# Modulation vectors of a two-layer trunk: TensorE sums over partitions replaced by multiply-and-sum instructions of VectorE

## The chip, the cores and the metric

The kernel runs on one core of one Trainium2 chip. A core has TensorE (matrix products, with a weight load that overlaps them), VectorE and ScalarE (elementwise work), POOL (GpSimd) and the queue of SyncE (SP), which issues transfers. They work side by side and wait for each other through semaphores. The metric is the device time of one execution in microseconds. The kernel before took 1705.62 us (median of 3 runs, 1704.53 to 1706.0).

## The reference

The program is a trunk of two layers over 256 context tokens and 256 latent tokens of width 1024. Each layer is a half SwiGLU, a mixer (mLSTM and spatial gating in layer 0, windowed attention in layer 1) and another half SwiGLU. Every one of these is modulated: two conditioning vectors (`c_ctx` for the context tokens, `c` for the latent ones) go through Silu and a 1024 x 9216 matrix per layer, which gives nine vectors of 1024: shift, scale and gate for each of the three parts.

```python
def _modulation(s, w, b):
    m = s @ w + b
    return m.reshape(s.shape[0], N_MOD, 1, D_MODEL)

def _modulate(h, shift, scale):
    return _rms_norm(h) * (1.0 + scale) + shift

def _swiglu(h, w_in, w_out):
    g, u = jnp.split(h @ w_in, 2, axis=-1)
    return (jax.nn.silu(g) * u) @ w_out
...
    sc = jax.nn.silu(c)
    scc = jax.nn.silu(c_ctx)[None]
...
        mod = _modulation(sc, ada_w[layer], ada_b[layer])
        modc = _modulation(scc, ada_w[layer], ada_b[layer])
        h = h + 0.5 * mod[:, 2] * _swiglu(_modulate(h, mod[:, 0], mod[:, 1]), ...)
```

All arithmetic is in fp32. The gates `mod[:, 2]` and `mod[:, 8]` carry a factor 0.5; the scales `mod[:, 1]`, `[:, 4]` and `[:, 7]` carry a 1 added. In layer 1 the context tokens end after the attention, so its vectors 5 to 8 are needed for `c` alone.

## The kernel before

The order of all instructions is written out by hand: a Python class, `Trunk`, emits them in the order in which each engine is to run them. Activations lie with features in partitions and 512 tokens along the row (256 context, 256 latent).

**Weights.** A weight unit is 128 x 1024 numbers (eight 128 x 128 blocks). `pump` streams units in pairs, 1 MB at a time, on SP's queue into a ring of three tiles `raw`, and three more, `rawx`, while there is room. `prep` splits a unit into two parts for a three-product scheme: ScalarE rounds it (`wh`, L259), VectorE takes the rest (`wl`, L243). Both have five buffers. `unit` then issues 24 matmuls, three for each of the eight blocks (L415 to L417). After every second block it calls `sub`.

**SwiGLU.** `ffn` runs three parts of up to eight column blocks `f`. For each `f` there are two units of the first matrix, a Silu on ScalarE (`sg`), a product on VectorE (`hd`), and a split of it into `HH` (ScalarE) and `HL` (VectorE). The part ends with eight units of the second matrix, added into the stream `H` with the gate (L625). The first four units of a SwiGLU, those of `f` 0 and 1, are computed together by `start` or `split_start`.

**Modulation vectors.** The first two vectors of layer 0 are computed on TensorE at the start (`ada`, items "s"). The other 32 items, of 512 outputs each, are spread over the first three half SwiGLUs by `make_ada`. Their weights travel in the same stream, two pieces of 1 MB an item; a piece holds 512 of the 1024 inputs, inputs in partitions and outputs along the row. `sub` calls `vada`, which holds a credit: `vrate` is added at each call (1.0 beside the first matrix, 0.5 beside the second), and one VectorE step costs 1.0. `vload` defines the steps: for each block of 128 inputs and each vector, one multiply-add of 512 columns into the accumulator `va` (L322, the first block L324), with one number of the Silu of `c` per partition. That leaves 128 partial sums per output, one in each partition. `total` sums them on TensorE with a matrix of ones (`pva`, L337), four matmuls for an item; ScalarE copies the result out (L341), and `finish` transposes it on VectorE (L344) and adds the bias with the factor 0.5 (L347). Results go to `mods`.

**POOL** holds a short queue: the masks' load and cast (L500, L501), the powers of the RMS norms (L528, L637 and others) and two more loads (L817, L1208).

Of the kernel before, what the change touches and what calls it, by code (L numbers as in the profile page):

```python
# [9 lines left out]
F32 = mybir.dt.float32  # L10
F32R = mybir.dt.float32r
BF16 = mybir.dt.bfloat16
# [134 lines left out]
class Trunk:  # L147
    def __init__(self, ctx, tc, a):
        self.tc, self.nc, self.a, self.ctx = tc, tc.nc, a, ctx
        self.V, self.S, self.G, self.M = tc.nc.vector, tc.nc.scalar, tc.nc.gpsimd, tc.nc.tensor  # L150
        self.cp = ctx.enter_context(tc.tile_pool(name="cp", bufs=1))
        self.ring = ctx.enter_context(tc.tile_pool(name="ring", bufs=RING))
        self.tp = ctx.enter_context(tc.tile_pool(name="tp", bufs=5))
        self.pp = ctx.enter_context(tc.tile_pool(name="pp", bufs=8, space=PSUM))
        self.dma_ptr = 0
        self.left = [len(v) if k == "u" else 1 for k, v, _, _ in GROUPS]
        self.raw = {}
        self.slot = {}
        self.live = [0, 0]
        self.extra = None  # L160
        self.xs = ExitStack()
        self.where = {}
        for g, (k, v, _, _) in enumerate(GROUPS):
            if k == "u":
                c = 0
                for i in v:
                    self.where[i] = (g, c)
                    c += unit_cols(UNITS[i])
            else:
                self.where[("a",) + v] = (g, 0)  # L170
        self.prep_ptr = 0
        self.half = None
        self.done_ptr = 0
        self.w = {}
        self.pe = [n for n, it in enumerate(ADA) if it[0] != "v"]
        self.ve = [(n, p) for n, it in enumerate(ADA) if it[0] == "v" for p in range(2)]
        self.vops = []
        self.vrate = self.credit = 0.0
        self.folds = []
        self.folded = set()  # L180
        self.posts = []
        self.bg = []
        self.subs = 0
        self.soon = []
        self.rs = {}
        self.adds = []
# [105 lines left out]

    def vada(self):
        self.credit = min(self.credit + self.vrate, 2.0)
        while self.credit >= 1.0:
            if not self.vops:
                if not self.ve:
                    return
                n, p = self.ve[0]
                g = self.where["a", n, p][0]  # L300
                if ADA[n][1][p] > self.done_ptr or g not in self.raw:
                    return
                self.ve.pop(0)
                self.vload(n, p, g)
            self.vops.pop(0)()
            self.credit -= 1.0

    def vload(self, n, p, g):
        V, M = self.V, self.M
        _, _, l, j, c0, w = ADA[n]  # L310
        ss = (1,) if l == 1 and j >= 5 else (0, 1)
        if p == 0:
            self.acc = self.vpool.tile([128, 2, 512], F32, tag="va", name="va", bufs=2)
        acc = self.acc
        raw = self.raw[g]

        def step(x, s):
            k = 4 * p + x
            c = self.SC[:, k, s:s + 1]
            src = raw[:, 512 * x:512 * x + 512]  # L320
            if k:
                V.scalar_tensor_tensor(acc[:, s], src, c, acc[:, s], ALU.mult, ALU.add)  # L322
            else:
                V.tensor_scalar(acc[:, s], src, c, None, ALU.mult)  # L324
            if x == 3 and s == 1:
                self.used(g)
                if p == 1:
                    self.later(wait, wait, total)

        def wait():  # L330
            pass

        def total():
            ps = self.bank("pva")
            sn = len(ss)
            for q in range(4):
                M.matmul(ps[32 * q:32 * q + 32, 0:128 * sn], lhsT=self.ONE[:, 0:32],  # L337
                         rhs=acc[:, ss[0]:2].rearrange("p s (k c) -> p s k c", c=128)[:, :, :, 32 * q:32 * q + 32],
                         start=True, stop=True, skip_group_check=True)
            t0 = self.tmp("va0")  # L340
            self.S.copy(t0[:, 0:128 * sn], ps[:, 0:128 * sn])  # L341

            def finish():
                V.transpose(t0[:, 256:256 + 128 * sn], t0[:, 0:128 * sn])  # L344
                self.folded.add((l, j, c0))
                ks = slice(c0 // 128, (c0 + w) // 128)
                V.scalar_tensor_tensor(  # L347
                    self.MOD[l, j][:, ks, ss[0]:2],
                    t0[:, 256:256 + 128 * sn].rearrange("p (s k m) -> p k s m", s=sn, k=4)[:, :, :, 0], 0.5 if j in (2, 8) else 1.0,
                    self.AB[:, l, j, ks].unsqueeze(2).to_broadcast([128, 4, sn]), ALU.mult, ALU.add)  # L350

            self.later(finish)

        self.vops.extend(lambda x=x, s=s: step(x, s) for x in range(4) for s in ss)

    def later(self, *fns):
        for i, fn in enumerate(fns):
# [102 lines left out]
    def setup(self):  # L460
        nc, a, V, S = self.nc, self.a, self.V, self.S
        cp = self.cp
        self.SM = cp.tile([128, S_N], F32, name="SM")
        self.C = cp.tile([128, C_N], F32, name="C")
        self.A = [None] * KT
        self.SS = cp.tile([128, 512], F32, name="SS")
        self.AX = cp.tile([128, KT, 256], F32, name="AX")
        self.SC = cp.tile([128, KT, 32], F32, name="SC")
        self.ONE = cp.tile([128, 128], F32, name="ONE")
        self.NHF = cp.tile([128, 4], F32, name="NHF")  # L470
        self.IDB = cp.tile([128, 128], BF16, name="IDB")
        self.MKB = cp.tile([128, 2, 128], BF16, name="MKB")
        mods = cp.tile([128, 18, KT, 2], F32, name="mods")
        self.H = cp.tile([128, KT, 512], F32, name="H")
        self.NH = cp.tile([128, KT, 512], F32R, tag="NH", name="NH")
        self.X = [[self.NH[:, k] for k in range(KT)], [None] * KT]
        self.MOD = {(l, j): mods[:, 9 * l + j] for l in range(2) for j in range(9)}
        nc.sync.dma_start(self.SM, a["small"])
        xv = a["xt"].rearrange("(k p) t -> p k t", p=128)
        for k in range(0, KT, 2):  # L480
            nc.sync.dma_start(self.H[:, k:k + 2, :], xv[:, k:k + 2, :])
        nc.sync.dma_start(self.C, a["const"])
        self.widen("f00")
        V.memset(self.ONE, 1.0)
        V.memset(self.NHF, -0.5)
        V.memset(self.SC, 0.0)
        S.activation(self.SC[:, :, 0:2], self.SM[:, S_C:S_C + 16].rearrange("p (k s) -> p k s", s=2), AF.Silu)
        self.AB = self.SM[:, S_AB:S_AB + 144].rearrange("p (l j t) -> p l j t", l=2, j=9)
        V.tensor_scalar(self.AB[:, :, 1::3, :], self.AB[:, :, 1::3, :], 1.0, None, ALU.add)
        V.tensor_scalar(self.AB[:, :, 2::6, :], self.AB[:, :, 2::6, :], 0.5, None, ALU.mult)  # L490
        self.ID = self.C[:, C_ID:C_ID + 128]
        self.heat(HEAT[0])
        for k in range(KT):
            self.add_squares()
            self.square(k, 0, 512)
        V.tensor_copy(self.IDB, self.ID)
# [225 lines left out]
    def ffn(self, l, i, c0, js, jc, jg):  # L722
# [8 lines left out]
        with self.tc.tile_pool(name=f"ffn{l}{i}", bufs=1) as fp:  # L731
            HH = fp.tile([128, 8, n], F32R, name="HH")
            HL = fp.tile([128, 8, n], F32R, name="HL")
            self.vpool = fp
            hs = [[t[:, k] for k in range(8)] for t in (HH, HL)]
            tag = f"f{l}{i}"
            c1 = c0 and c0 - 2
# [15 lines left out]
            ready = dict(zip(STARTS[tag][0], pss))  # L753
            if mid:
                self.masks()

            def proj(u):
                if u in ready:
# [9 lines left out]
            for p, (fa, fb) in enumerate(PARTS):  # L768
                self.vrate = 1.0
                for f in range(fa, fb):  # L770
                    ug, uu = ("wi", l, i, 0, f), ("wi", l, i, 1, f)
                    pg = proj(ug)
                    sg = self.tmp("sg")
# [739 lines left out]
def pack(w):  # L1513
    flat = np.empty(WFLAT, np.float32)
    for k, v, cols, off in GROUPS:
        dst = flat[off:off + cols * 128].reshape(128, cols)
        if k == "u":
            c = 0
            for i in v:
                n = unit_cols(UNITS[i])  # L1520
                b = unit_block(UNITS[i], w)
                dst[:, c:c + n].reshape(b.shape)[:] = b
                c += n
        else:
            _, _, l, j, c0, width = ADA[v[0]]
            kn = 2048 // width
            m = w["ada_w"][l][128 * kn * v[1]:128 * kn * (v[1] + 1), 1024 * j + c0:1024 * j + c0 + width]
            dst.reshape(128, kn, width)[:] = m.reshape(kn, 128, width).transpose(1, 0, 2)
# [15 lines left out]
    mix[:, M_MN:M_MN + 512] = w["mlstm_norm"][0].reshape(1, 512)  # L1544
    xt = np.concatenate([w["ctx"][0].T, w["x"][0].T], axis=1)
    const, late = constants()
    return {"w": flat, "small": small, "mix": mix, "xt": np.ascontiguousarray(xt), "const": const, "late": late}


# [13 lines left out]
```

## Time and profile before

| | |
|---|---|
| runs, median | 1705.62 us |
| profiled execution, its time | 1705.36 us |
| its span, first to last instruction | 1703.2 us |
| TensorE busy | 1689.5 us (99%) |
| VectorE busy | 1143.2 us (67%) |
| ScalarE busy | 652.9 us (38%) |
| POOL busy | 24.7 us (1%) |
| read from HBM | 245.28 MB |
| granted TensorE clock | 0.998 |

A line of a group gives line, engine, operation, written and read tiles, shape and count, then busy time in us and the mean of one in ns, then the idle time of that engine just before them and what ended it. A line of the timeline gives start and duration in us; where several alike are merged, the duration is that of all. Starts of matmuls show more than their durations, since one starts before the last has ended.

### The profile page before, as it was taken

Reading aid. Unit: us, or ns where it says so; the run is one execution under the profiler, and the core shown is the slowest. Engines: PE = TensorE matmul, PEld = TensorE weight load, DVE = VectorE, ACT = ScalarE, POOL = GpSimd, SP = SyncE. Lnnn points to the kernel's source line nnn. Section 1 sums busy time; section 2 is a strip of 40 time slices with the busy share of each in tenths; the row PEclk is TensorE's granted clock in tenths of the full one; section 3 lists DMA queues with packets and bytes.
Section 4 is the critical chain, followed back from the end, with each engine's and each line's share of the span. In section 5 each row is a group of like instructions: output and inputs, shape, how many; then the busy total and the mean of one; then the engine's idle time right before and its main releaser. Section 6 shows DMA issues by size and latency. Waiting matters only on the chain.

```text
span 1703.2 us, 23813 instructions
## 1 busy us (share of the span) xinstructions
PE 1689.5 (99%) x9702; PEld 1439.8 (85%) x9702; DVE 1143.2 (67%) x1997; ACT 652.9 (38%) x1083; POOL 24.7 (1%) x29
## 2 busy tenths in 40 slices
PE   9999999999999999999999999999999999999998
PEld 6788888889788898888888898888888897799998
DVE  6876786767877757767766377646654377576765
ACT  4421222235545454222222353213212357664444
POOL 0000000000000100000000000000000000000000
PEclk9999999999999999999999999999999999999999
DMA  9654454541211334534544144444443031165440
GB/s 372 230 183 144 179 187 148 177 169 32 88 50 52 114 121 174 192 129 183 198 148 149 50 149 174 182 157 167 186 148 124 25 132 51 51 247 192 180 161 26
DMA packets 36462, 247.87 MB, mean 146 GB/s; under 512 B 4000, under 2 KB 4256, under 8 KB 8960
## 3 DMA queue, kind: packets, MB, share of 16 engines
q1 hardware_dynamic: 35792, 244.57, 39.3%
q8 instruction: 76, 1.25, 0.3%
q0 software_dynamic: 272, 1.25, 0.2%
q10 hardware_dynamic: 288, 0.52, 0.1%
q14 instruction: 34, 0.28, 0.0%
HBM read 245.28 MB, written 1.05 MB: 145 GB/s over the span
## 4 chain that ended last, share of the span: by engine, by line
PE 96%; DVE 2%; ACT 1%; DMA 0%; issue 0%; SPq 0%; POOLq 0%; ACTq 0%; DVEq 0%
PE bank L415 25%; PE bank L417 25%; PE bank L416 25%; PE bank L710 5%; PE bank L444 4%; PE bank L1124 1%; PE bank L1126 1%; PE bank L1125 1%; PE pva L337 1%; PE pov L1315 1%; PE psc L1279 1%; PE ppt L1300 1%; PE pada L383 0%; PE pO L1006 0%; DMA H<-xt 0%; PE pB L1008 0%
## 5 line engine op out<-in xcount | busy, mean ns | idle before, releaser
L415 PE MATMUL bank<-NH,wh 128*128 128x512 f32 (+2 forms) x1416 | 513.2, 362 | 0.0
L417 PE MATMUL bank<-NH,wl 128*128 128x512 f32 (+2 forms) x1416 | 506.7, 358 | 1.4 <-DVE wl L243 1.4
L416 PE MATMUL bank<-NL,wh 128*128 128x512 f32 (+2 forms) x1384 | 497.3, 359 | 0.0
L415 PEld LDWEIGHTS bank<-NH,wh 128*128 128x128 f32 x1416 | 266.2, 188 | 47.1 <-issue 9.0
L417 PEld LDWEIGHTS bank<-NH,wl 128*128 128x128 f32 x1416 | 266.1, 188 | 41.3 <-DVE wl L243 1.8
L416 PEld LDWEIGHTS bank<-NL,wh 128*128 128x128 f32 x1384 | 260.2, 188 | 38.3
L259 ACT CAST wh<-raw 128x1024 fp32r<-128x1024 f32 (+1 forms) x207 | 212.5, 1029 | 153.1 <-PE bank L416 99.8
L415 PE MATMUL bank<-HH,wh 128*128 128x512 f32 (+1 forms) x776 | 269.3, 347 | 0.0
L416 PE MATMUL bank<-HL,wh 128*128 128x512 f32 (+1 forms) x776 | 268.1, 345 | 0.1
L417 PE MATMUL bank<-HH,wl 128*128 128x512 f32 (+1 forms) x776 | 268.0, 345 | 0.0
L243 DVE TENSOR_TENSOR wl<-raw,wh 128x1024 fp32r<-128x1024 f32 (+1 forms) x207 | 246.9, 1197 | 18.6 <-ACT wh L259 18.6
L625 DVE SCALAR_TENSOR_TENSOR H<-bank,mods,H 128x256 f32<-128x256 f32 x192 | 86.6, 480 | 174.3 <-PE bank L417 171.7
L790 ACT CAST HH<-hd 128x512 fp32r<-128x512 f32 (+1 forms) x88 | 49.9, 567 | 313.3 <-DVE hd L789 278.6
L259 ACT CAST wh<-rawx 128x1024 fp32r<-128x1024 f32 (+1 forms) x118 | 119.8, 1016 | 118.3 <-PE bank L416 102.2
L415 PEld LDWEIGHTS bank<-HH,wh 128*128 128x128 f32 x776 | 146.9, 189 | 20.2 <-issue 2.5
L416 PEld LDWEIGHTS bank<-HL,wh 128*128 128x128 f32 x776 | 147.0, 189 | 18.0 <-DVE HL L791 0.3
L417 PEld LDWEIGHTS bank<-HH,wl 128*128 128x128 f32 x776 | 147.0, 189 | 17.9
L322 DVE SCALAR_TENSOR_TENSOR va<-rawx,SC,va 128x512 f32<-128x512 f32 x228 | 159.6, 746 | 1.2
L789 DVE TENSOR_TENSOR hd<-sg,bank 128x512 f32<-128x512 f32 x66 | 45.3, 687 | 155.1 <-PE bank L417 149.7
L243 DVE TENSOR_TENSOR wl<-rawx,wh 128x1024 fp32r<-128x1024 f32 (+1 forms) x118 | 139.0, 1181 | 3.6 <-ACT wh L259 3.6
L322 DVE SCALAR_TENSOR_TENSOR va<-raw,SC,va 128x512 f32<-128x512 f32 x164 | 114.0, 745 | 0.4
L780 ACT ACTIVATE sg<-bank 128x512 f32<-128x512 f32 x66 | 39.5, 598 | 149.2 <-PE bank L417 148.8
(289 smaller groups left out, 1753.4 us busy)
## 6 DMA issues: line engine op xcount, KB each, us to landing
raw<-w SPq DMA_DIRECT2D x123, 1024.0 KB, 4.8
rawx<-w SPq DMA_DIRECT2D x91, 1024.0 KB, 4.9
rawx<-w SPq DMA_DIRECT2D x7, 768.0 KB, 4.4
raw<-w SPq DMA_DIRECT2D x6, 768.0 KB, 4.2
raw<-w SPq DMA_DIRECT2D x3, 896.0 KB, 4.5
H<-xt SPq DMA_DIRECT2D x4, 512.0 KB, 6.0
rawx<-w SPq DMA_DIRECT2D x2, 896.0 KB, 4.5
raw<-w SPq DMA_DIRECT2D x2, 512.0 KB, 9.8
```

Source lines behind the costliest of these rows:

```text
L243: self.V.tensor_tensor(lo[:, :n], src, hi[:, :n].bitcast(F32), ALU.subtract)
L259: self.S.copy(hi[:, :n], src)
L322: V.scalar_tensor_tensor(acc[:, s], src, c, acc[:, s], ALU.mult, ALU.add)
L415: self.M.matmul(ps, lhsT=wh, rhs=xh, start=start, stop=False)
L416: self.M.matmul(ps, lhsT=wh, rhs=xl, start=False, stop=False)
L417: self.M.matmul(ps, lhsT=wl, rhs=xh, start=False, stop=stop)
L444: self.M.matmul(pss[i][:, 0:hi - lo], lhsT=w[wi][:, c:c + 128], rhs=(xh, xl)[xi][kt][:, lo:hi], start=n == b == 0, stop=n == 3 and b == 5)
L625: self.V.scalar_tensor_tensor(self.H[:, m, q], ps[:, c - lo:c - lo + 256], gate[:, m, c // 256:c // 256 + 1], self.H[:, m, q], ALU.mult, A ...
L710: self.M.matmul(pss[i][:, q], lhsT=lhs, rhs=rhs, start=n == b == 0, stop=n == 3 and b == 5)
L780: S.activation(sg, pg, AF.Silu)
L789: V.tensor_tensor(hd, sg, pu, ALU.mult)
L790: S.copy(HH[:, f - fa], hd[:, 0:n])
```

## The change

The items that VectorE computes get another layout. A piece now holds 256 outputs, all 1024 inputs of each: outputs lie in partitions, inputs along the row. The Silu of both conditioning vectors must then lie along the row too, the same in all partitions: `vectors` loads them with one broadcast of 1 MB on POOL's queue into `cb`, a tile of each of the first three half SwiGLUs, and `silu` applies Silu to it in place, at `f` 1. VectorE's step is one `tensor_tensor_reduce`: 1024 columns of weights times 1024 columns of `cb`, times 0.5 for the gates, summed along the row on top of the bias, into one column of `mods`. The products themselves go to `dump` (bf16) and are not used. The 1 of the scales, formerly part of the bias for all vectors, is added at the end of an item. The sum on TensorE, its copy, transpose and last step are gone. A step costs two credits, and there are half as many; an item's result is there with its last step.

```diff
     def vada(self):
         self.credit = min(self.credit + self.vrate, 2.0)
-        while self.credit >= 1.0:
+        if not self.lit:
+            return
+        while self.credit >= 2.0:
             if not self.vops:
...
             self.vops.pop(0)()
-            self.credit -= 1.0
+            self.credit -= 2.0
 
     def vload(self, n, p, g):
...
         def step(x, s):
-            k = 4 * p + x
-            c = self.SC[:, k, s:s + 1]
-            src = raw[:, 512 * x:512 * x + 512]
-            if k:
-                V.scalar_tensor_tensor(acc[:, s], src, c, acc[:, s], ALU.mult, ALU.add)
-            else:
-                V.tensor_scalar(acc[:, s], src, c, None, ALU.mult)
-            if x == 3 and s == 1:
+            k = c0 // 128 + 2 * p + x
+            self.V.tensor_tensor_reduce(
+                self.dump, raw[:, 1024 * x:1024 * x + 1024], self.cb[:, s], 0.5 if j in (2, 8) else 1.0,
+                self.AB[:, l, j, k:k + 1], ALU.mult, ALU.add, self.MOD[l, j][:, k, s:s + 1])
+            if x == s == 1:
                 self.used(g)
                 if p == 1:
-                    self.later(wait, wait, total)
...
-        def total():
-            ps = self.bank("pva")
-            sn = len(ss)
-            for q in range(4):
-                M.matmul(ps[32 * q:32 * q + 32, 0:128 * sn], lhsT=self.ONE[:, 0:32],
-                         rhs=acc[:, ss[0]:2].rearrange("p s (k c) -> p s k c", c=128)[:, :, :, 32 * q:32 * q + 32],
-                         start=True, stop=True, skip_group_check=True)
-            t0 = self.tmp("va0")
-            self.S.copy(t0[:, 0:128 * sn], ps[:, 0:128 * sn])
...
-        self.vops.extend(lambda x=x, s=s: step(x, s) for x in range(4) for s in ss)
+                    self.folded.add((l, j, c0))
+                    if j % 3 == 1:
+                        t = self.MOD[l, j][:, c0 // 128:c0 // 128 + 4, ss[0]:2]
+                        self.V.tensor_scalar(t, t, 1.0, None, ALU.add)
+
+        self.vops.extend(lambda x=x, s=s: step(x, s) for x in range(2) for s in ss)
+
+    def vectors(self, pool):
+        self.lit = False
+        self.cb = pool.tile([128, 2, D], F32, name="cb")
+        self.G.dma_start(self.cb, self.a["cond"].unsqueeze(0).to_broadcast([128, 2, D]))
+        self.dump = self.tp.tile([128, D], BF16, tag="ada1", name="dump", bufs=2)
+
+    def silu(self):
+        for s in range(2):
+            self.S.activation(self.cb[:, s], self.cb[:, s], AF.Silu)
+        self.lit = True
...
-        V.tensor_scalar(self.AB[:, :, 1::3, :], self.AB[:, :, 1::3, :], 1.0, None, ALU.add)
+        V.tensor_scalar(self.AB[:, 0, 1, :], self.AB[:, 0, 1, :], 1.0, None, ALU.add)
...
-            self.vpool = fp
+            if not first and not c0:
+                self.vectors(fp)
...
             if mid:
                 self.masks()
+                self.vectors(fp)
...
                 for f in range(fa, fb):
+                    if f == 1 and not c0:
+                        self.silu()
...
+            if mode == "v":
+                m = w["ada_w"][l][:, 1024 * j + c0 + 256 * v[1]:1024 * j + c0 + 256 * v[1] + 256]
+                dst.reshape(128, 2, D)[:] = m.reshape(D, 2, 128).transpose(2, 1, 0)
+                continue
...
+    cond = np.stack([w["c_ctx"], w["c"][0]])
```

On TensorE, in the first half SwiGLU, a sum stands between two triples of ordinary matmuls. Before:

```order
L415 MATMUL bank<-NH,wh 128x512
L416 MATMUL bank<-NL,wh 128x512
L417 MATMUL bank<-NH,wl 128x512
L337 MATMUL pva<-va,ONE 32x256 x4
L415 MATMUL bank<-NH,wh 128x512
L416 MATMUL bank<-NL,wh 128x512
```

In the changed kernel no row names `pva`, here or at the 31 other places; the triples (now L401 to L403) follow each other directly.

On VectorE, the stretch of one `f` of the first half SwiGLU, from `hd` on. The names: `raw` and `rawx` hold streamed weights, `SC` the Silu of the conditioning with inputs in partitions, `SM` the small constants with the bias. Before:

```order
L789 TENSOR_TENSOR hd<-sg,bank 128x512
L791 TENSOR_TENSOR HL<-hd,HH 128x512
L243 TENSOR_TENSOR wl<-rawx,wh 128x1024
L322 SCALAR_TENSOR_TENSOR va<-raw,SC,va 128x512 x4
L243 TENSOR_TENSOR wl<-raw,wh 128x1024
L322 SCALAR_TENSOR_TENSOR va<-raw,SC,va 128x512 x4
```

Now (each multiply-and-sum is two rows, the second reads the accumulator):

```order
L779 TENSOR_TENSOR hd<-sg,bank 128x512
L781 TENSOR_TENSOR HL<-hd,HH 128x512
L244 TENSOR_TENSOR wl<-rawx,wh 128x1024
L318 ISA dump,mods<-rawx,cb,SM 128x1024
L318 ISA mods 128x1
L318 ISA dump,mods<-rawx,cb,SM 128x1024
L318 ISA mods 128x1
L244 TENSOR_TENSOR wl<-rawx,wh 128x1024
L318 ISA dump,mods<-rawx,cb,SM 128x1024
L318 ISA mods 128x1
L318 ISA dump,mods<-rawx,cb,SM 128x1024
L318 ISA mods 128x1
```

Four multiply-adds of 512 columns behind each `wl` have become two multiply-and-sums of 1024 columns with their reads.

On ScalarE, at the beginning of the first half SwiGLU, the Silu of the vectors stands between the work of `f` 0 and that of `f` 1. Now:

```order
L260 CAST wh<-raw 128x1024 x4
L770 ACTIVATE sg<-bank 128x512
L780 CAST HH<-hd 128x512
L339 ACTIVATE cb<-cb 128x1024 x2
L770 ACTIVATE sg<-bank 128x512
L780 CAST HH<-hd 128x512
```

Before, these rows stood there without the one of `cb`; the 32 copies of `pva` to `va0` further on are gone. The load that this activation reads is issued by POOL behind the masks' cast (in the other two half SwiGLUs, ahead of the power of the norm's second half).

More of the change, by code (lines that the diff above doesn't have):

```diff
@@ L305, in vada @@
             self.vops.pop(0)()
-            self.credit -= 1.0
+            self.credit -= 2.0
     def vload(self, n, p, g):
-        V, M = self.V, self.M
         _, _, l, j, c0, w = ADA[n]
         ss = (1,) if l == 1 and j >= 5 else (0, 1)
-        if p == 0:
-            self.acc = self.vpool.tile([128, 2, 512], F32, tag="va", name="va", bufs=2)
-        acc = self.acc
         raw = self.raw[g]
         def step(x, s):
-            k = 4 * p + x
-            c = self.SC[:, k, s:s + 1]
-            src = raw[:, 512 * x:512 * x + 512]
-            if k:
-                V.scalar_tensor_tensor(acc[:, s], src, c, acc[:, s], ALU.mult, ALU.add)
-            else:
-                V.tensor_scalar(acc[:, s], src, c, None, ALU.mult)
-            if x == 3 and s == 1:
+            k = c0 // 128 + 2 * p + x
@@ L326, in step @@
+            self.V.tensor_tensor_reduce(
+                self.dump, raw[:, 1024 * x:1024 * x + 1024], self.cb[:, s], 0.5 if j in (2, 8) else 1.0,
+                self.AB[:, l, j, k:k + 1], ALU.mult, ALU.add, self.MOD[l, j][:, k, s:s + 1])
+            if x == s == 1:
                 self.used(g)
                 if p == 1:
-                    self.later(wait, wait, total)
-        def wait():
-            pass
-        def total():
-            ps = self.bank("pva")
-            sn = len(ss)
-            for q in range(4):
-                M.matmul(ps[32 * q:32 * q + 32, 0:128 * sn], lhsT=self.ONE[:, 0:32],
-                         rhs=acc[:, ss[0]:2].rearrange("p s (k c) -> p s k c", c=128)[:, :, :, 32 * q:32 * q + 32],
-                         start=True, stop=True, skip_group_check=True)
-            t0 = self.tmp("va0")
[L341 to L352, printed above, removed]
@@ L354, in vload @@
-        self.vops.extend(lambda x=x, s=s: step(x, s) for x in range(4) for s in ss)
+                    self.folded.add((l, j, c0))
[4 more added lines that the diff above has]
+    def vectors(self, pool):
+        self.lit = False
+        self.cb = pool.tile([128, 2, D], F32, name="cb")
+        self.G.dma_start(self.cb, self.a["cond"].unsqueeze(0).to_broadcast([128, 2, D]))
+        self.dump = self.tp.tile([128, D], BF16, tag="ada1", name="dump", bufs=2)
@@ L1524, in pack @@
         else:
-            _, _, l, j, c0, width = ADA[v[0]]
+            mode, _, l, j, c0, width = ADA[v[0]]
+            if mode == "v":
+                m = w["ada_w"][l][:, 1024 * j + c0 + 256 * v[1]:1024 * j + c0 + 256 * v[1] + 256]
+                dst.reshape(128, 2, D)[:] = m.reshape(D, 2, 128).transpose(2, 1, 0)
+                continue
             kn = 2048 // width
@@ L1546, in pack @@
     const, late = constants()
-    return {"w": flat, "small": small, "mix": mix, "xt": np.ascontiguousarray(xt), "const": const, "late": late}
+    cond = np.stack([w["c_ctx"], w["c"][0]])
+    return {"cond": cond, "w": flat, "small": small, "mix": mix, "xt": np.ascontiguousarray(xt), "const": const, "late": late}
 def kernel(**inputs):
```

## The prediction, made before the changed kernel was run

> **What bounds the kernel now.** I read the page's busy shares and its chain of waits first, then the list of TensorE's own waits, then the timeline of TensorE around the instructions that the change removes.
>
> ```profile
> PE 1689.5 (99%) x9702; PEld 1439.8 (85%) x9702; DVE 1143.2 (67%) x1997; ACT 652.9 (38%) x1083; POOL 24.7 (1%) x29
> ...
> PE 96%; DVE 2%; ACT 1%; DMA 0%; issue 0%; SPq 0%; POOLq 0%; ACTq 0%; DVEq 0%
> PE bank L415 25%; PE bank L417 25%; PE bank L416 25%; PE bank L710 5%; PE bank L444 4%; PE bank L1124 1%; PE bank L1126 1%; PE bank L1125 1%; PE pva L337 1%; PE pov L1315 1%; PE psc L1279 1%; PE ppt L1300 1%; PE pada L383 0%; PE pO L1006 0%; DMA H<-xt 0%; PE pB L1008 0%
> ```
>
> TensorE is busy for 99% of the span and is 96% of the chain that ended last. The matmul that this change deletes, `pva` at L337, stands in that chain with 1%. The next view lists who TensorE waited for; its two longest rows are these.
>
> ```profile
> PE bank L444 <- ACT NH L585: 1.7, 4, 1.1
> PE bank L417 <- DVE wl L243: 1.4, 1, 1.4
> ```
>
> Hardly any time of TensorE is waiting, so time is gained only by giving it less to do, and lost only if a change makes it wait. `pva` has no row there: its matmuls cost TensorE their own time, not a wait. How much is read from the timeline of TensorE around one of the 32 sums over partitions, the second of the first half-SwiGLU; the columns are start and duration in us.
>
> ```profile
> 102.30 0.39 PE L417 MATMUL bank<-NH,wl 128*128 128x512 f32 x1
> 102.53 0.39 PE L415 MATMUL bank<-NH,wh 128*128 128x512 f32 x1
> 102.75 0.39 PE L416 MATMUL bank<-NL,wh 128*128 128x512 f32 x1
> 102.98 0.39 PE L417 MATMUL bank<-NH,wl 128*128 128x512 f32 x1
> 103.30 0.64 PE L337 MATMUL pva<-va,ONE 128*32 128x256 f32 x8
> 103.87 0.50 PE L415 MATMUL bank<-NH,wh 128*128 128x512 f32 x1
> ...
> 105.36 0.39 PE L415 MATMUL bank<-NH,wh 128*128 128x512 f32 x1
> ```
>
> Durations of matmuls overlap, so starts are compared. Ordinary matmuls start every (102.98 - 102.30) / 3 = 0.227 us. From 102.98 to 105.36 seven of them start (103.87 is the first, five follow it in the rows left out up to 105.13, 105.36 is the last): 7 x 0.227 = 1.59 us of 2.38. The remaining **0.79 us** is the price of one sum.
>
> **The change, part by part.** First, what TensorE loses. The instructions of `pva` are counted by form in the view of that tile; behind it stands the same piece of timeline for a narrow sum, of layer 1's later vectors, which only the latent tokens need.
>
> ```profile
> L337 PE MATMUL pva<-va,ONE x256: 272/379/404, 80.7 to 1291.3; 128*32 128x256 f32 x96, 128*32 128x128 f32 x32
> L341 ACT COPY va<-pva x32: 265/372/373, 81.5 to 1291.6; 128x256 f32<-128x256 f32 x24, 128x128 f32<-128x128 f32 x8
> ```
>
> ```profile
> 1290.78 0.39 PE L417 MATMUL bank<-NH,wl 128*128 128x512 f32 x1
> 1291.10 0.43 PE L337 MATMUL pva<-va,ONE 128*32 128x128 f32 x8
> ...
> 1292.95 0.39 PE L415 MATMUL bank<-NH,wh 128*128 128x512 f32 x1
> ```
>
> There are 24 wide sums and 8 narrow ones (the copies at L341 count them). The narrow one: seven ordinary starts again between 1290.78 and 1292.95, 2.17 - 1.59 = 0.58 us. So TensorE is relieved of 24 x 0.79 + 8 x 0.58 = 19.0 + 4.6 = **23.6 us**. All of it lies on the path, because TensorE has nothing to wait for on either side.
>
> Second, what VectorE gets. For a wide item (512 outputs, two conditioning vectors) it now issues 14 multiply-adds and 2 multiplies of 512 columns, a transpose and a small last step. After the change it issues 8 multiply-and-sums over 1024 columns, each followed by a read of the accumulator into one column of `mods`. Neither form is in this trace; these rows bound it.
>
> ```profile
> L322 DVE SCALAR_TENSOR_TENSOR va<-raw,SC,va 128x512 f32<-128x512 f32 x164 | 114.0, 745 | 0.4
> L243 DVE TENSOR_TENSOR wl<-raw,wh 128x1024 fp32r<-128x1024 f32 x191 | 231.8, 1217 | 18.2 <-ACT wh L259 18.2
> L1019 DVE TENSOR_TENSOR NM<-NM,pO 128x129 f32<-128x129 f32 x24 | 6.5, 288 | 10.0 <-ACT NM L1012 9.9
> L1284 DVE TENSOR_REDUCE st<-psc 128x1 f32<-128x512 f32 x32 | 21.7, 679 | 5.2 <-PE psc L1281 5.0
> L874 DVE TENSOR_TENSOR_SCAN rb<-ONE,Z 36x128 f32<-36x128 f32 x4 | 1.4, 398 | 0.0
> L785 DVE COPY bu<-bank 128x1 f32<-128x1 f32 x22 | 3.4, 156 | 19.5 <-PE bank L417 19.5
> ```
>
> Lower end: a product of two fp32 rows of 1024 takes 1.217 us (L243), a one-column operation 0.156 us (L785): 1.37 us a pair. Upper end: the scan also feeds each result into the next. From L243 and L1019 a two-input operation costs (1217 - 288) / (1024 - 129) = 1.04 ns an element on 154 ns; the scan costs (398 - 154) / 128 = 1.91 ns, which for 1024 gives 2.11 us, with the read 2.27 us. I take 1.4 us, near the lower end: the row nearest to a sum along the row is the reduction L1284, whose 679 ns for 512 columns is no more than a two-input operation of that width by the same line (154 + 512 x 1.04 = 686 ns).
>
> Whether VectorE can afford that is read from one steady cycle between two sums: four units of 24 matmuls, one wide item. The first row gives TensorE, weight loads, VectorE and ScalarE busy; the other two are from VectorE's timeline inside it.
>
> ```profile
> 102.98:125.54 22.56, 22.56 (x105) 18.10 (x104) 17.89 (x28) 6.59 (x9) 0.00 (x0) 1.00 0.52 187
> ```
>
> ```profile
> 111.44 0.69 DVE L789 TENSOR_TENSOR hd<-sg,bank 128x512 f32<-128x512 f32 x1 [2.38 <-PE bank L417]
> 112.81 0.69 DVE L791 TENSOR_TENSOR HL<-hd,HH 128x512 fp32r<-128x512 f32 x1 [0.69 <-ACT HH L790]
> ```
>
> VectorE idles 22.56 - 17.89 = 4.67 us per cycle, some of it waiting for TensorE's results: it is ahead. After the change the cycle is 96 x 0.227 = 21.8 us. In it VectorE has 4 `wl` (4 x 1.217), 2 `hd` and 2 `HL` (4 x 0.69) and 2 waits for `HH` (2 x 0.69): 9.0 us. That leaves 12.8 us for 8 multiply-and-sums, **1.6 us** each. At 1.4 us they need 11.2 and stay hidden; at 2.27 they need 18.2 and do not. The ten small additions of 1 to the scale vectors (128x8, some 0.16 us each) are hidden likewise. ScalarE loses 32 copies and gains six activations; it is at 38%.
>
> [...]
>
> Third, the new load and activation. In each of three half-SwiGLUs POOL issues a 1 MB broadcast of the conditioning vectors, and ScalarE applies Silu to it in place before the second `sg`. The tightest place is the first one; DMA rows are median us from issue to landing.
>
> ```profile
> 47.65 0.39 POOL L501 CAST MKB<-mk 128x256 bf16<-128x256 f32 x1 [4.55 <-DMA mk<-late]
> ...
> raw<-w SPq DMA_DIRECT2D x123, 1024.0 KB, 4.8
> mk<-late POOLq DMA_DIRECT2D x1, 128.0 KB, 5.2
> ```
>
> ```profile
> 55.74 0.62 ACT L790 CAST HH<-hd 128x512 fp32r<-128x512 f32 x1 [0.75 <-DVE hd L789]
> 56.27 0.59 ACT L780 ACTIVATE sg<-bank 128x512 f32<-128x512 f32 x1
> ...
> L259 ACT CAST wh<-raw 128x1024 fp32r<-128x1024 f32 x191 | 199.3, 1047 | 153.1 <-PE bank L416 99.8 <-PE bank L444 22.9 <-PE bank L710 19.7
> ...
> 51.14 3.50 DVE L243 TENSOR_TENSOR wl<-raw,wh 128x1024 fp32r<-128x1024 f32 x3 [0.25 <-ACT wh L259]
> ...
> 61.10 1.21 DVE L243 TENSOR_TENSOR wl<-raw,wh 128x1024 fp32r<-128x1024 f32 x1
> ```
>
> The broadcast goes behind the mask's cast, which ends at 48.04; with 5.2 us (the slower row) it lands near 54, and ScalarE reaches the Silu at about 56.3. The two activations of 1024 columns cost about 2 x 1.05 us (L259 is ScalarE's nearest row of that width, 1047 ns). Behind them in ScalarE's queue stand `sg`, `HH` and further casts; VectorE's `HL`, multiply-and-sums and the next `wl` wait for those. Who needs that next: three `wl` were made at 51.14, for the three units that TensorE starts at 54.8 and works on for 3 x 24 x 0.227 = 16.3 us, so the fourth, now done at 62.31, is wanted at 71.1. Against these 8.8 us stand 2.1 of Silu and some 0.5 of dearer VectorE steps: nothing is lost, and about 6 us of a late landing would still be covered. In the other two half-SwiGLUs the load has the whole start for its landing. There it passes in POOL's queue ahead of a small power whose result TensorE wants.
>
> ```profile
> 1373.04 0.60 POOL L1208 DMA_DIRECT2D TR<-late  x1 [5.64 <-ACT AX L550]
> ...
> 635.18 0.70 POOL L637 TENSOR_TENSOR r<-ms,NHF 128x2 f32<-128x2 f32 x1 [11.24 <-DVE ms L636]
> 1006.68 0.70 POOL L637 TENSOR_TENSOR r<-ms,NHF 128x2 f32<-128x2 f32 x1 [9.09 <-DVE ms L636]
> ```
>
> POOL is idle for 9.09 and 11.24 us ahead of those powers, and an issue holds it 0.60 us: hidden. Without that cover an issue costs 0.6 us each, 1.2 in all. The order in which weights and modulation pieces stream on SP's queue does not change; 3 MB more in 248 is far below what the queues have spare (0.52 busy in the cycle above).
>
> **Sum.** The profiled execution took 1705.36 us, 1703.2 of span and 2.2 around it. Less 23.6 it is 1681.8. The median of the runs, 1705.62, lies 0.3 above, so I forecast **1682 us**, 1.4% faster.
>
> **Rivals.** (1) Slower: the multiply-and-sum runs like the scan, at 2.27 us. VectorE then sets the pace wherever wide items run beside the first matrix of a SwiGLU. The cycle becomes 8 x 2.27 + 9.0 = 27.2 us instead of 21.8. Of the 24 wide items 20 lie there (ten, eight and two in the three half-SwiGLUs; the other four run beside the second matrix at half the rate), so 20 x 5.4 = 108 us are lost: 1790. It decides from 1.6 us on. For it speaks the scan's row, against it L1284, where a running sum costs no more per column than a product. (2) No change: at a price between, the loss eats the gain; 23.6 / 20 = 1.18 us a cycle means 1.74 us a pair, and 1.70 to 1.79 us gives a time near 1702 to 1709. Only a narrow stretch between the bounds does that. (3) Faster, but less: the first broadcast lands late, beyond the 6 us, or the Silu holds `HL` and the first multiply-and-sums so that a SwiGLU's first `wl` is missing. 16 us from issue to landing instead of 5.2 would cost about 5 us, three such places 15: 1684 to 1697. Against it speaks that every load of 1 MB here lands in about 4.8 us. That the sums might stay is excluded: no `pva` row is left in the order of TensorE.
>
> **How the numbers follow.** The forecast gets 0.82, (1) 0.07, (2) 0.04, (3) 0.07. The price of one sum is known to about 0.01 us, so below the forecast there is little room: 1679 allows 3 us for waits that vanish with the sums. Above, I take in most of (3): 1692. The bounds of the unknown price up to 1.6 us change nothing in the time and are inside; (1) and (2), 0.11 together, are left out. A difference of 0.2% (3.4 us) is about what a measurement of this kernel can tell from no change: faster 0.89, same 0.04, slower 0.07.
>
> **What would show it right or wrong.** Right: the span shorter by 23 to 24 us, no `pva` on TensorE, ordinary starts 0.227 us apart right through the first matrices, the multiply-and-sum with its read at 1.3 to 1.6 us, and TensorE's list of waits about as short as before. Wrong: TensorE waiting for `wl`, `hd` or `HL` of VectorE for whole microseconds per unit (rival 1 or 2), or one long wait near 55 to 75 us, 660 or 1030 us behind the broadcast (rival 3).

## The result and the profile after

The changed kernel takes 1682.65 us (median of 4 runs, 1680.38 to 1684.46); the kernel before took 1705.81 us beside it (4 runs, 1704.53 to 1708.07). The ratio is 0.986, with a 95% interval of 0.9845 to 0.9879: 1.4% faster, where 1682 was forecast. The profiled execution took 1682.59 us with a span of 1680.7 us, 22.5 less than before.

From the page of the changed kernel: the engines' busy times, and the chain of work that ended last, by engine and by line.

```profile
PE 1666.1 (99%) x9446; PEld 1437.5 (86%) x9446; DVE 1120.1 (67%) x1943; ACT 648.0 (39%) x1057; POOL 26.4 (2%) x32
...
PE 96%; DVE 2%; ACT 1%; DMA 0%; issue 0%; SPq 0%; POOLq 0%; ACTq 0%; DVEq 0%
PE bank L401 25%; PE bank L402 25%; PE bank L403 25%; PE bank L696 6%; PE bank L430 4%; PE bank L1116 1%; PE bank L1114 1%; PE bank L1115 1%; PE pov L1305 1%; PE psc L1269 1%; PE ppt L1290 1%; PE pada L369 0%; PE pO L996 0%; DMA H<-xt 0%; PE pB L998 0%; PE pss L621 0%
```

TensorE has 256 rows of matmuls fewer (the profile has two for each of the 128 matmuls of the sums), its busy time has fallen by 23.4 us, and it is still 96% of the chain. `pva` is gone from the chain and nothing new stands in its place. Its three longest waits, in the list of TensorE's waits of the changed kernel (total us, times, longest):

```profile
PE bank L430 <- ACT NH L571: 1.7, 4, 1.1
PE pss L508 <- ACT sq L491: 1.7, 1, 1.7
PE bank L403 <- DVE wl L244: 1.4, 1, 1.4
```

No VectorE step of the new kind is waited for: the rows for `NH` and `wl` are those of before under new line numbers. The row for `sq` is a wait at the start, 1.1 us before, and 0.6 to 2.8 us in the variants below. In TensorE's timeline of the changed kernel, the place that held the sum now reads:

```profile
102.12 0.39 PE L401 MATMUL bank<-NH,wh 128*128 128x512 f32 x1
...
102.80 0.39 PE L401 MATMUL bank<-NH,wh 128*128 128x512 f32 x1
```

With two between them that are left out, the starts are (102.80 - 102.12) / 3 = 0.227 us apart.

**Where the 22.5 us come from.** Every half SwiGLU and mixer begins with an RMS norm, whose matmul `pR` spreads a result over the partitions. Its starts in TensorE's timeline cut the program into stages. Of the six, the first two and the last are shown, first of the kernel before, then of the changed one; the table has the differences between all six.

```profile
16.43 1.51 PE L534 MATMUL pR<-C,r 128*128 128x128 f32 x8
...
398.76 0.63 PE L643 MATMUL pR<-C,r 128*128 128x128 f32 x4
...
1515.02 0.61 PE L643 MATMUL pR<-C,r 128*128 128x128 f32 x4
```

```profile
17.47 1.59 PE L520 MATMUL pR<-C,r 128*128 128x128 f32 x8
...
390.23 0.63 PE L629 MATMUL pR<-C,r 128*128 128x128 f32 x4
...
1492.19 0.61 PE L629 MATMUL pR<-C,r 128*128 128x128 f32 x4
```

| stage | before, us | after, us | shorter by | sums removed, at the forecast's prices |
|---|---|---|---|---|
| start | 16.43 | 17.47 | -1.04 | none |
| first half SwiGLU | 382.33 | 372.76 | 9.57 | 12 wide: 12 x 0.79 = 9.5 |
| mLSTM layer | 226.06 | 226.06 | 0.00 | none |
| second half SwiGLU | 372.93 | 364.94 | 7.99 | 10 wide: 7.9 |
| third half SwiGLU | 369.79 | 363.49 | 6.30 | 2 wide, 8 narrow: 1.6 + 4.6 = 6.2 |
| attention | 147.48 | 147.47 | 0.01 | none |
| last half SwiGLU | 188.2 | 188.5 | -0.3 | none |

The time is gone from exactly the stages that held sums, and from each by its number of sums. About 1 us of it was lost again elsewhere: the start took 1.04 us longer. Windows of the same stretch, before and then after (busy of TensorE, weight loads, VectorE, ScalarE and POOL, then the granted clock, the DMA share and GB/s):

```profile
11.70:18.60 6.90, 6.90 (x60) 5.46 (x64) 1.60 (x7) 0.37 (x1) 1.01 (x1) 0.75 1.01 413
```

```profile
11.70:18.60 6.90, 6.90 (x40) 5.41 (x40) 0.77 (x3) 0.37 (x1) 1.01 (x1) 0.51 1.02 418
```

In this execution the clock stood at half for nearly all of the 6.9 us, before for half of them. The order of TensorE's work is the same there, and in the two variants with further broadcasts below, which hold the whole change, the first `pR` came at 15.9 and 15.4 us: it differs from execution to execution.

### The profile page after: what moved, and what is told of

The parts are those of the page before. It is cut to its first block, busy times and chain, and to the rows that moved or that the text cites. A ratio compares the mean times of both kernels' runs of the same rounds, so it can differ in the third digit from the quotient of the medians.

```text
span 1680.7 us, 23242 instructions
## 1 busy us (share of the span) xinstructions
PE 1666.1 (99%) x9446; PEld 1437.5 (86%) x9446; DVE 1120.1 (67%) x1943; ACT 648.0 (39%) x1057; POOL 26.4 (2%) x32
## 3 DMA queue, kind: packets, MB, share of 16 engines
q8 instruction: 74, 1.21, 0.3%
## 4 chain that ended last, share of the span: by engine, by line
PE 96%; DVE 2%; ACT 1%; DMA 0%; issue 0%; SPq 0%; POOLq 0%; ACTq 0%; DVEq 0%
PE bank L401 25%; PE bank L402 25%; PE bank L403 25%; PE bank L696 6%; PE bank L430 4%; PE bank L1116 1%; PE bank L1114 1%; PE bank L1115 1%; PE pov L1305 1%; PE psc L1269 1%; PE ppt L1290 1%; PE pada L369 0%; PE pO L996 0%; DMA H<-xt 0%; PE pB L998 0%; PE pss L621 0%
## 5 line engine op out<-in xcount | busy, mean ns | idle before, releaser
L401 PE MATMUL bank<-NH,wh 128*128 128x512 f32 (+2 forms) x1416 | 510.1, 360 | 0.0
L403 PE MATMUL bank<-NH,wl 128*128 128x512 f32 (+2 forms) x1416 | 506.5, 358 | 1.4 <-DVE wl L244 1.4
L403 PEld LDWEIGHTS bank<-NH,wl 128*128 128x128 f32 x1416 | 266.1, 188 | 40.8 <-DVE wl L244 1.8
L401 PEld LDWEIGHTS bank<-NH,wh 128*128 128x128 f32 x1416 | 266.2, 188 | 39.2
L401 PE MATMUL bank<-HH,wh 128*128 128x512 f32 (+1 forms) x776 | 268.5, 346 | 0.0
L403 PE MATMUL bank<-HH,wl 128*128 128x512 f32 (+1 forms) x776 | 267.9, 345 | 0.0
L318 DVE CUSTOM_DVE_ANT_0 dump<-rawx,cb,SM 128x1024 bf16<-128x1024 f32 x128 | 164.0, 1281 | 1.9
L401 PEld LDWEIGHTS bank<-HH,wh 128*128 128x128 f32 x776 | 146.9, 189 | 18.0
L403 PEld LDWEIGHTS bank<-HH,wl 128*128 128x128 f32 x776 | 147.0, 189 | 17.8
L318 DVE CUSTOM_DVE_ANT_0 dump<-raw,cb,SM 128x1024 bf16<-128x1024 f32 x96 | 123.0, 1281 | 1.4
```

Source lines behind the costliest of these rows:

```text
L318: self.V.tensor_tensor_reduce(self.dump, raw[:, 1024 * x:1024 * x + 1024], self.cb[:, s], 0.5 if j in (2, 8) else 1.0, self.AB[:, l, j, k: ...
L401: self.M.matmul(ps, lhsT=wh, rhs=xh, start=start, stop=False)
L403: self.M.matmul(ps, lhsT=wl, rhs=xh, start=False, stop=stop)
```

## Experiments

The theory is the forecast's: the gain is TensorE's own time for the sums, and what VectorE, ScalarE and POOL do in their place is hidden. One rival says that part of the gain comes from the other layout (fewer instructions of VectorE, fewer waits). The other says that the hidden parts are close to being bounds, so that the gain was luck.

### Is it the sums, and nothing but the sums?

First, the sums alone out of the kernel before. Its VectorE still does the old multiply-adds; what it leaves out is the sum, so its modulation vectors are not those of the reference.

```diff
 def total():                                  # in the kernel before
-    ps = self.bank("pva")
...
-    for q in range(4):
-        M.matmul(ps[32 * q:32 * q + 32, 0:128 * sn], lhsT=self.ONE[:, 0:32], ...)
     t0 = self.tmp("va0")
-    self.S.copy(t0[:, 0:128 * sn], ps[:, 0:128 * sn])
+    self.S.copy(t0[:, 0:128 * sn].rearrange("p (s c) -> p s c", s=sn), acc[:, ss[0]:2, 0:128])
```

> The kernel before, with VectorE's multiply-adds, ScalarE's copy, the transpose and the last step all kept, but without the four matmuls of each sum over partitions (the copy reads the accumulator instead, so the modulation vectors are partial sums of one partition's inputs: the sum is left out). Theory 1 (the gain is the sums' own time on TensorE, 24 x 0.79 + 8 x 0.58 = 23.6 us): 1705.6 - 23.6 = 1682, the same as the changed kernel. Theory 2 (part of the gain comes from VectorE or ScalarE, which no longer stand still for the sum, or from the cheaper layout): between 1685 and 1700, clearly slower than the changed kernel.

Measured: 1681.81 us (1680.72 to 1682.98), against 1706.23 before: 0.9857, 0.984 to 0.9873. With the old steps on VectorE and no sum, the time is that of the changed kernel within 1 us.

Second, the sums alone into the changed kernel. Their result is not read.

```diff
                 if p == 1:
                     self.folded.add((l, j, c0))
+                    self.later(wait, wait, total)
...
+        def total():
+            ps = self.bank("pva")
+            sn = len(ss)
+            for q in range(4):
+                self.M.matmul(ps[32 * q:32 * q + 32, 0:128 * sn], lhsT=self.ONE[:, 0:32],
+                              rhs=self.C[:, 0:128 * sn], start=True, stop=True, skip_group_check=True)
```

> The changed kernel, with four matmuls of the sum's shape put back on TensorE for each item, at the place of the old sum and on constant data; nothing reads them. Theory 1 (TensorE's own time is the whole gain): the gain is gone, 1682.6 + 23.6 = 1706. Theory 2 (a part of the gain is VectorE's or ScalarE's): 1690 to 1703.

Measured: 1706.39 us, ratio 0.9997 (0.9987 to 1.0006): the whole gain is gone again. The group of `pva` in this variant, and TensorE's timeline around one sum:

```profile
L337 PE MATMUL pva<-C,ONE 128*32 128x256 f32 (+1 forms) x256 | 18.7, 364 | 0.0
```

```profile
103.62 0.39 PE L414 MATMUL bank<-NH,wl 128*128 128x512 f32 x1
103.94 0.64 PE L337 MATMUL pva<-C,ONE 128*32 128x256 f32 x8
104.51 0.50 PE L412 MATMUL bank<-NH,wh 128*128 128x512 f32 x1
```

The step from 103.62 to 104.51 is that of the kernel before (102.98 to 103.87): 0.89 us, whatever was summed. The group shows 18.7 us of busy time, but the sums cost 23.7 (1706.39 - 1682.65); the rest lies in the wider gaps around them, which is why starts were compared and not durations. The starts of `pR` say the same stage by stage. Without the sums, and with the old layout, the second and third half SwiGLU take 364.93 and 363.49 us, as in the changed kernel (364.94 and 363.49); with the sums put back into the new layout they take 372.93 and 369.79, as in the kernel before. The first rival falls: the layout itself is worth nothing measurable.

### How much room had VectorE?

In the changed kernel a step is one product and one read. The group with the tiles `rawx` (the 96 with `raw` have the same mean) and the read, then a piece of VectorE's timeline where it works without a wait:

```profile
L318 DVE CUSTOM_DVE_ANT_0 dump<-rawx,cb,SM 128x1024 bf16<-128x1024 f32 x128 | 164.0, 1281 | 1.9
...
L318 DVE DVE_READ_ACCUMULATOR2_ANT mods<- 128x1 f32 x224 | 18.6, 83 | 0.0
```

```profile
62.28 1.28 DVE L318 CUSTOM_DVE_ANT_0 dump<-raw,cb,SM 128x1024 bf16<-128x1024 f32 x1
63.49 0.09 DVE L318 DVE_READ_ACCUMULATOR2_ANT mods<- 128x1 f32 x1
63.61 1.29 DVE L318 CUSTOM_DVE_ANT_0 dump<-raw,cb,SM 128x1024 bf16<-128x1024 f32 x1
...
64.82 1.22 DVE L244 TENSOR_TENSOR wl<-raw,wh 128x1024 fp32r<-128x1024 f32 x1
```

Two steps take 64.82 - 62.28 = 2.54 us, **1.27 us** a step. The forecast put the room at 1.6 us and the price of crossing it at 20 cycles. Three variants make the step dearer by a further product of 128, 384 or 1024 columns, whose result nobody reads, to find where VectorE begins to set the pace:

```diff
             self.V.tensor_tensor_reduce(
                 self.dump, raw[:, 1024 * x:1024 * x + 1024], self.cb[:, s], ...)
+            self.V.tensor_tensor(self.dump[:, 0:W], raw[:, 1024 * x:1024 * x + W],
+                                 self.cb[:, s, 0:W], ALU.mult)      # W = 128, 384, 1024
```

> The changed kernel, with one more product of 128 columns (not used) behind each multiply-and-sum. A step of VectorE costs 1.33 us in the changed kernel (1.281 and 0.084, less overlap); here some 0.25 more, 1.58. Theory (a cycle of four units has room for 8 steps of 1.6 us; below that VectorE stays hidden): no change, 1682 to 1684. Rival (VectorE's price counts at any size, because results come later): 224 x 0.25 = 56 us spread over the items, 1700 or more.

> The same with a product of 384 columns, some 0.52 us: 1.85 us a step, beyond the room. Theory: a cycle becomes 8 x 1.85 + 9.0 = 23.8 us instead of 21.8; 20 cycles, 40 us: 1723 (1705 to 1735, as the room is known to about 0.1 us a step). Rival (the room is larger, as VectorE catches up beside the second matrix): 1682 to 1690.

> The same with a product of 1024 columns, 1.2 us: 2.53 us a step, dearer than the upper end of the prediction (2.27). Theory: a cycle becomes 8 x 2.53 + 9.0 = 29.2 us, 7.4 more; 20 cycles: 148 us, 1831. This is the first rival of the prediction made real.

Measured, against 1705.85 us before in the same session:

| W | further product, ns | time, us | ratio and interval |
|---|---|---|---|
| 128 | 292 | 1682.85 | 0.987 (0.9855 to 0.9884) |
| 384 | 558 | 1713.42 | 1.004 (1.0026 to 1.0055) |
| 1024 | 1225 | 1819.88 | 1.0668 (1.0652 to 1.0684) |

VectorE's own pace shows in the starts of consecutive products `hd`, one for each `f`, where VectorE is behind. TensorE's pace for an `f` is 48 matmuls of 0.227 us, 10.88 us. VectorE's timeline of the changed kernel where it catches up after the first Silu, then of the variants with 128, 384 and 1024 columns:

```profile
69.63 0.68 DVE L779 TENSOR_TENSOR hd<-sg,bank 128x512 f32<-128x512 f32 x1
...
78.95 0.68 DVE L779 TENSOR_TENSOR hd<-sg,bank 128x512 f32<-128x512 f32 x1
```

```profile
69.05 0.68 DVE L780 TENSOR_TENSOR hd<-sg,bank 128x512 f32<-128x512 f32 x1
...
79.67 0.68 DVE L780 TENSOR_TENSOR hd<-sg,bank 128x512 f32<-128x512 f32 x1
```

```profile
108.76 0.68 DVE L780 TENSOR_TENSOR hd<-sg,bank 128x512 f32<-128x512 f32 x1
...
120.45 0.68 DVE L780 TENSOR_TENSOR hd<-sg,bank 128x512 f32<-128x512 f32 x1
```

```profile
104.84 0.68 DVE L780 TENSOR_TENSOR hd<-sg,bank 128x512 f32<-128x512 f32 x1
...
119.20 0.68 DVE L780 TENSOR_TENSOR hd<-sg,bank 128x512 f32<-128x512 f32 x1
```

The paces are 9.32, 10.62, 11.69 and 14.36 us. An `f` holds four steps, so the changed kernel's work without them is 9.32 - 4 x 1.27 = 4.24 us, and the room is (10.88 - 4.24) / 4 = **1.66 us** a step. This room is worked out, not measured; what the runs show is that it lies between 1.60 and 1.86. A step of the three variants costs (pace - 4.24) / 4: 1.60, 1.86 and 2.53 us. The first stays just under the room and costs nothing that the medians show; the second is past it and eats the gain, 30.8 us slower than the changed kernel's 1682.65; the third costs 137 us. In the variant with 384 columns the excess of 11.69 - 10.88 = 0.81 us holds for some 36 `f`, 20 in the first half SwiGLU and 16 in the second: 29 us. By the starts of `pR` these two stages are 15.7 and 14.5 us longer than in the changed kernel, 30.2 together. With 1024 columns it is 3.48 us for the same 36, 125 us, and 13.7 more by which the third half SwiGLU was longer: 139.

The expectation counted 20 cycles of two `f`, two of them in the third half SwiGLU, and 4.5 us of other work for an `f` in place of 4.24; that is why it came out at 1723 and 1831, some 10 us high in both. In the variant with 384 columns, moreover, the third half SwiGLU lost nothing: VectorE was behind there too, but caught up before TensorE had to wait.

The variant with 128 columns is not quite free. Its second half SwiGLU takes 366.61 us, 1.7 more than in the changed kernel, and its list of TensorE's waits has a new row:

```profile
PE bank L402 <- ACT HH L781: 0.9, 1, 0.9
```

A SwiGLU begins with VectorE behind, and at 10.62 us an `f` it gains only 0.26 us on TensorE's 10.88: there it did not catch up before the second matrix. In the first and the third half SwiGLU nothing was lost.

How the lag reaches TensorE was not foreseen. TensorE's waits in the variant with 384 columns, then with 1024:

```profile
PE bank L402 <- ACT HH L781: 19.3, 5, 7.3
```

```profile
PE bank L402 <- ACT HH L781: 79.7, 11, 13.0
PE bank L404 <- DVE wl L244: 23.8, 16, 2.4
```

With 384 columns the lag is not spread over the units. The buffers of `wl` and the order of TensorE's units take it up over a whole part, and it comes out as one wait for `HH` in each of five parts, ahead of the second matrix, which needs the last `hd` at once. With 1024 columns they do not suffice: TensorE also waits for `wl`, 16 times and not once.

### How late may the broadcast land?

In the changed kernel POOL issues the first broadcast at 49.12, and ScalarE waits for its landing. POOL's timeline, ScalarE's, and the row of the transfers (KB each, median us from issue to landing):

```profile
49.12 0.57 POOL L334 DMA_DIRECT2D cb<-cond  x1
...
57.78 2.01 ACT L339 ACTIVATE cb<-cb 128x1024 f32<-128x1024 f32 x2 [0.35 <-DMA cb<-cond]
...
cb<-cond POOLq DMA_DIRECT2D x3, 1024.0 KB, 8.6
```

It lands after some 8.6 us, not 5.2, and the Silu waits 0.35 us. So the cover is used here already, and two variants measure how much of it is left: the first broadcast is issued once or twice more, into the same tile, so that the Silu comes later.

```diff
             if mid:
                 self.masks()
                 self.vectors(fp)
+                for _ in range(N):                       # N = 1, 2
+                    self.G.dma_start(self.cb, self.a["cond"].unsqueeze(0).to_broadcast([128, 2, D]))
```

> The changed kernel, with the broadcast of the conditioning vectors in the first half SwiGLU issued twice into the same tile, the second behind the landing of the first; so it lands some 8 us later (the changed kernel's landed 8.6 us after its issue). Theory 1 (three units of split weights cover the wait): in the changed kernel the fourth wl is done at 66.0 and wanted at about 72.7, so 6.6 us are covered and TensorE stands still for 1 to 2 us at most: 1683 to 1685. Rival (the Silu and VectorE's queue behind it are on the path at once): 8 us longer, 1690 to 1691.

> The same with the broadcast issued three times, so that it lands some 16 us late. Theory 1: 16 - 6.6 = 9 us of standing still on TensorE, waiting for wl, near 73 us of the span: 1690 to 1694. Rival (the delay is on the path from the start): 1698 to 1699. If nothing is lost, the cover is larger than the count of split units says.

Measured: 1682.12 us with two loads (0.9856, 0.9841 to 0.987), 1687.92 us with three (0.9889, 0.9874 to 0.9904), against 1706.23 before. ScalarE's timeline of the variant with two loads, and of the one with three:

```profile
61.35 2.01 ACT L339 ACTIVATE cb<-cb 128x1024 f32<-128x1024 f32 x2 [5.80 <-DMA cb<-cond]
```

```profile
66.48 2.01 ACT L339 ACTIVATE cb<-cb 128x1024 f32<-128x1024 f32 x2 [10.77 <-DMA cb<-cond]
```

ScalarE waits 5.80 us in the first and TensorE has no new wait. In the second it waits 10.77, and TensorE's timeline has this:

```profile
70.70 0.39 PE L402 MATMUL bank<-NL,wh 128*128 128x512 f32 x1
74.80 0.50 PE L403 MATMUL bank<-NH,wl 128*128 128x512 f32 x1 [3.71 <-DVE wl L244]
...
75.84 0.63 PE L403 MATMUL bank<-NH,wl 128*128 128x512 f32 x1
76.27 0.63 PE L401 MATMUL bank<-NH,wh 128*128 128x512 f32 x1
...
78.78 0.39 PE L401 MATMUL bank<-NH,wh 128*128 128x512 f32 x1
```

The wait is for `wl`, at 71, both as the forecast's rival (3) had it. The cover is 10.77 - 3.71 = 7.06 us from the moment ScalarE is ready. Both times came out lower than expected (1683 to 1685, 1690 to 1694): the first lateness of 5.80 us lies inside this cover, and the third load made the Silu 10.77 us late and not 16. POOL's timeline in this variant shows the three loads. POOL waited 8.60 us for the first to land before it issued the second, and 4.64 for the second before the third:

```profile
47.28 0.54 POOL L334 DMA_DIRECT2D cb<-cond  x1
56.42 0.54 POOL L745 DMA_DIRECT2D cb<-cond  x1 [8.60 <-DMA cb<-cond]
61.59 0.53 POOL L745 DMA_DIRECT2D cb<-cond  x1 [4.64 <-DMA cb<-cond]
```

The time lost is 1687.92 - 1682.65 = 5.3 us, or 5.8 against the variant with two loads, more than the wait of 3.71 us. The rest is in the rows behind it: from 74.80 to 78.78 ten matmuls start, 0.40 us apart, where 2.27 us would have done, 1.7 us more.

## Why the prediction was right

**What TensorE loses** (24 x 0.79 + 8 x 0.58 = 23.6 us, all on the path): right, and shown twice. The stages with sums are shorter by 9.57, 7.99 and 6.30 us, 23.9 together; adding the sums alone gives 23.7 back, removing them alone gives the whole gain. Span and sum differ by 1.04 us at the start, where the clock was slower, and 0.3 at the end, where the change does nothing.

**What VectorE gets** (1.37 to 2.27 us a pair, 1.4 taken): right in the choice, and the price is below the lower bound: 1.27 us a step. The time of the kernel does not tell this, since any price up to the room gives the same; the rows do. The product takes 1.281 us, 0.064 more than the plain product of that width at L243. The read was the term mis-sized: 0.083 us, not the 0.156 of a one-column operation, and most of it lies beside the end of the product (63.49 is 1.21 us behind the product's start). The sum along the row costs next to nothing here, as the reduction L1284 had suggested and the scan had not. With two fp32 sources and an accumulator the product takes 1.25 ns a column (1281 / 1024).

**The room of 1.6 us**: right, 1.66 by the paces, with 1.60 a step all but hidden (1.7 us lost in one stage) and 1.86 no longer. VectorE's row in a steady cycle of the changed kernel shows it ahead:

```profile
190.00:211.76 21.76, 21.76 (x97) 18.02 (x97) 17.30 (x25) 6.23 (x8) 0.00 (x0) 1.00 0.55 194
```

It is busy 17.30 of 21.76 us, before 17.89 of 22.56.

**Rivals (1) and (2)**: their mechanism exists, their condition was not met. A step of 1.86 us gave 1713 us and one of 2.53 us 1820; by rival (1)'s own formula, 20 x (8 x price + 9.0 - 21.8) added to 1682, 1.86 us gives 1724 and 2.53 us 1831. It is too dear by about 10 us for the reasons given above, 4.24 us against 4.5 and, at 1.86 us, the third half SwiGLU that lost nothing. Rival (2) has a slip of its own: by that formula 1.70 to 1.79 us give 1698 to 1712, not 1702 to 1709.

**The new load and Silu**: right in the result, wrong in the landing. "Lands near 54", from the mask's 5.2 us, was 57.7: it took 8.6 us. The forecast read the queues' spare room from a steady cycle with a DMA share of 0.52, but in the window of this load, 49.1 to 57.7, the share is 0.99, and in those of the other two 0.99 (623.2 to 634.7) and 0.77 (986.7 to 993.4). So the load did arrive late, by 0.35 us behind ScalarE, and only the cover, put at about 6 us and measured at 7.06, made it free. Rival (3) overstated its price: by the forecast's own times a landing 16 us after the issue at 48.04 is 7.7 us behind ScalarE at 56.3, so 6 us of cover leave less than 2 us and not 5; and the other two loads, by its own words, have a whole start for their landing. The two activations took 2.01 us, forecast 2.1. **POOL's issues** were hidden: in the second and third half SwiGLU POOL still idles 2.87 and 2.90 us between the issue and the power behind it, both stages are shorter by all of their sums, and no new wait of TensorE appeared at a norm.

## What to carry to other kernels

Where one engine is busy 99% of the span, price a change by that engine's starts before and after the piece that goes, not by the durations of the instructions: here the group's 18.7 us of busy time stood for 23.7 us of time. Moving the work to another engine is free up to a room that can be computed from one steady cycle (here 1.66 us a step; 1.60 cost 1.7 us in one stage and nothing elsewhere, 1.86 ate the gain), and beyond it the loss grows by every cycle, so know the price on both sides of it, and leave some spare for what the engine has to catch up. Here a late input cost nothing up to its cover and then its lateness and something on top, so work out the cover for each new transfer by who is queued behind it.

## What the runs showed of the hardware that was not expected

A wait of TensorE can cost more than its length. In the variant with three loads the wait of 3.71 us was followed by a stretch at half clock. The granted clock in a window behind it, in that variant (columns as in the windows above):

```profile
75.00:78.00 3.00, 3.00 (x9) 2.31 (x9) 2.96 (x4) 0.00 (x0) 0.00 (x0) 0.55 0.65 221
```

The matmuls start 0.43 us apart there (75.84 to 76.27) in place of 0.227, for about 3.4 us, and then the clock is back (1.00 from 79.50 to 80.50). The wait of 1.4 us that stands in the lists of waits is not followed by this: in the changed kernel it ends at 444.8, and the window behind it is at full clock (1.00). TensorE's timeline, and the window:

```profile
444.86 0.50 PE L403 MATMUL bank<-NH,wl 128*128 128x512 f32 x1 [1.36 <-DVE wl L244]
```

```profile
444.80:449.00 4.20, 4.14 (x24) 3.67 (x25) 3.71 (x6) 3.73 (x9) 0.00 (x0) 1.00 0.24 55
```

In between, the variant with 1024 columns has seven waits for `wl` of 2.39 to 2.43 us. Behind five of them a slow stretch comes, behind two none. One of each kind, in TensorE's timeline of that variant, and windows of it: the one that ends where the clock falls, the one behind it, and one that begins inside the second wait:

```profile
122.45 0.50 PE L404 MATMUL bank<-NH,wl 128*128 128x512 f32 x1 [2.42 <-DVE wl L244]
...
264.77 0.50 PE L404 MATMUL bank<-NH,wl 128*128 128x512 f32 x1 [2.42 <-DVE wl L244]
```

```profile
120.20:123.60 3.40, 1.15 (x5) 0.96 (x6) 3.03 (x4) 2.71 (x4) 0.00 (x0) 1.00 0.99 320
123.60:127.00 3.40, 3.40 (x10) 2.62 (x9) 3.30 (x4) 0.00 (x0) 0.00 (x0) 0.50 0.77 296
263.55:270.35 6.80, 5.58 (x24) 4.43 (x24) 6.70 (x9) 1.68 (x3) 0.00 (x0) 1.00 0.74 288
```

Behind the first wait the clock is at half (0.50) from 123.60 to 127.0, 3.4 us that begin about 1 us after TensorE has begun again; behind the second it stays full (1.00). Both waits took 2.42 us, so their length alone does not decide whether the clock falls. What does, no run was made to find out.

So a lag of VectorE shows as more than the waits it makes. In the variant with 384 columns the waits for `HH` are 19.3 us of the 30.8 lost. The mean granted clock was 0.990 there and 0.997 in the changed kernel, which over 1712 us is up to 12 us more. VectorE's excess of 29 us nearly explains the whole loss by itself, so waits and slower clock are the two forms in which it shows on TensorE; that the clock added to it is not shown.

A further product of 128 columns costs 292 ns and one of 1024 columns 1225 ns, so a short one is mostly fixed cost, (1225 - 292) / 896 = 1.04 ns a column on 159 ns.

The same 1 MB broadcast needed 6.7 to 11.5 us in the changed kernel and about 5 us when it was repeated a few microseconds later (5.17 in the variant with three loads, from the issue at 56.42 to 61.59). There the DMA share was 0.99 while the first was under way (47.3 to 56.4) and 0.68 and 0.58 for the two repeats, so full DMA engines go with the slow landing; which transfers filled them was not tried.
